# Two mixers on one core: TensorE in program order in the woven stage, the products of head pairs alternated, modulation steps two by two

## The chip, the cores and the metric

The kernel runs on one core of one Trainium2 chip. The metric is the time of one execution in microseconds (us) on the device. Names of engines: PE is TensorE, DVE is VectorE, ACT is ScalarE, POOL is GpSimd, and SP is the engine whose queue issues most of the loads.

## The reference

Two layers of a diffusion backbone run over 256 context and 256 latent tokens of width 1024. Each layer has a mixer and a mixture of experts, both behind a modulated norm. What matters here is the mixer:

```
mod = silu(c) @ w_mod[l] + b_mod[l]                  # shifts, scales, gates; the same for c_ctx
p = modnorm(x, ...) @ w_in                           # one projection for both groups
A: q, k, v of 8 heads from low-rank parts, rotary on 32 of 96 dimensions
   s = q.k ; p = softmax(s * scale) ; o_att = p @ v  # context reads context, latents read both
B: state-space mixer, two directions, chunks of 128:
   states per chunk ; y = (C B^T * decay) @ (x dt) + C exp(acs) @ h_prev + D x
   o_ssd = rmsnorm(y * silu(z))
out = concat(o_att, o_ssd) @ w_out ; x = x + gate * out
```

In layer 0 both streams leave the mixer (four tiles of 128 queries). In layer 1 only the latents do (two tiles), and their queries read all 512 keys.

## The kernel before, in words

Each mixer first projects and convolves. Then comes the stage that the change is about: three generators are woven together by `weave`. Each yields a cost after every step, and the one whose summed cost over its weight (`ATT_W`, `SSD_W`, `MOD_W`) is smallest goes next.

- **Attention, `g_att`.** A unit is a head pair's half: group `a` of two heads, query tile `t`, head `e`. `qk_proj` (L749) makes kT and qT of a pair: L753 and L760 on PE, copied out on ACT and DVE (L754, L755, L762, L763). `scores` (L766) multiplies q and k on PE (L770), then runs the softmax: maximum on DVE (L772), exponential on ACT (L774), reciprocal and scale on DVE (L775, L776). `flip` (L779) transposes the probabilities on PE (L783) and copies them to pT on ACT (L785). `attend` (L788) multiplies v by pT on PE (L792), 2 products for 256 keys (tiles 0 and 1 of layer 0), 4 for 512. Head 0 writes partitions 0 to 63 of a PSUM tile `py`, head 1 partitions 64 to 127, and one DVE copy (L821) takes the tile out. With `LOOK = 3`, step n makes the scores of unit n, flips unit n-3 and attends unit n-4.
- **State space, `g_ssd`.** Six chunk states (L891 on POOL, products L894), then for each query tile: a product (L912), masks (L917), a decay matrix per half of the heads from a broadcast load on the SP queue into `ring` (L924; L930, L934 on DVE or POOL, L936 and L943 on ACT, L938 to L944 on DVE or POOL), products with the states (L953, L955), the main product (L960), gate and norm (L961 to L967), and transposes (L972, L974).
- **Modulation, `mods`.** A chain of `mod_group` (L269) for the later parts of this layer and `mod_norm1` (L212) for the next layer's first norm. `mod_group` reads a 1 MB piece of `w_mod` per step (tile `wl`, issued at L139 on the SP queue) and multiplies it in four groups of 32 columns (L303). It ends with transposes (L316). `mod_norm1` has eight blocks; each multiplies a 1 MB piece (L221), yields, and, after a DVE copy of the result to `mr` (L223), runs a small product with a selector (L227) and three DVE instructions (L228 to L230).

The weight pieces live in a pool of `WHB = 4` buffers of 1 MB. Until the last `qk_proj`, `wkv` and `wq` hold two of them. PSUM has two buffers each for scores (`sc`), transposes (`tp`) and other products (`bk`), and one each for `py` and `md` (the modulation).

The order in which a program issues is not always the order in which an engine runs it: outside a `manual_schedule` block a scheduler sets the order on each engine. Before the change, the woven stage stands outside of such a block, so the scheduler orders PE there. The other engines and the SP queue are the scheduler's in both kernels.

## Time and profile before

| | us |
|---|---|
| median of 3 runs | 1081.5 (1081.06 to 1082.82) |
| profiled execution | 1077.21 |
| its span | 1075.4 |
| PE busy | 954.0 (89%) |
| DVE busy | 610.3 (57%) |
| POOL busy | 354.6 (33%) |
| ACT busy | 335.1 (31%) |

The profiled execution is the one that every row below is from. Its own time is 1.8 us above its span. In rows of groups, the columns are line, engine, operation, names out<-in, shapes and count, then busy time and the mean of one in ns, then the idle time in front and who ended it. In timeline rows, a start and a duration come first; the busy durations of matmuls overlap each other, so what a block of products costs PE is the step from its start to the next row's start. A product of the program is two matmuls in the trace, a transpose one.

### The profile page before, as it was taken

The page shows a single profiled execution, that of the slowest core. Times are in us where ns is not written, and L with a number is a line of the kernel's source. Part 1 is how long each engine was busy: PE and PEld are TensorE (multiplying, and loading weights), DVE is VectorE, ACT ScalarE, POOL GpSimd, SP SyncE. Part 2 cuts the span into 40 slices and gives each one's busy share as a digit, 9 for nine tenths or more (in the row PEclk, how much of TensorE's full clock was granted, in tenths as well). Part 3 has the DMA queues.
Part 4 walks back from the last instruction along what each step waited for, and adds up shares of the span by engine and source line. Part 5 has one row for each costly group of instructions (what it writes and reads, how often), then busy time and mean ns, then how long its engine had stood idle before and what let it go on. Part 6 is the DMA issues. An engine that isn't in the chain of part 4 may idle for free. (4 is left out here: it accounts for less than half of the span.)

```text
span 1075.4 us, 14508 instructions
## 1 busy us (share of the span) xinstructions
PE 954.0 (89%) x5244; PEld 556.7 (52%) x5244; DVE 610.3 (57%) x1351; ACT 335.1 (31%) x688; POOL 354.6 (33%) x366
## 2 busy tenths in 40 slices
PE   5999999999996999999969979999999678877785
PEld 3678745667775444444424327683678434433331
DVE  4587089885687355656435667857886423323232
ACT  4365344453541111111102126543455111110111
POOL 2130134430355266667645650103331001112023
PEclk9999999999996999999989989999999598899699
DMA  9512387687567989799898625646496689999995
GB/s 380 188 42 76 143 312 253 255 301 267 220 178 284 378 360 405 317 418 417 360 375 329 268 79 194 236 156 258 178 326 236 229 335 395 420 419 387 391 418 208
DMA packets 54675, 306.21 MB, mean 285 GB/s; under 512 B 6168, under 2 KB 7064, under 8 KB 22976
## 3 DMA queue, kind: packets, MB, share of 16 engines
q1 hardware_dynamic: 49120, 288.10, 68.4%
q0 software_dynamic: 4224, 15.21, 4.4%
q10 hardware_dynamic: 1248, 1.86, 0.5%
q8 instruction: 44, 0.72, 0.3%
q14 instruction: 39, 0.32, 0.1%
HBM read 300.89 MB, written 4.26 MB: 284 GB/s over the span
## 5 line engine op out<-in xcount | busy, mean ns | idle before, releaser
L1669 POOL TENSOR_TENSOR xs<-xs,tmp 128x512 f32<-128x512 f32 x144 | 180.0, 1282 | 219.6 <-DVE tmp L1668 219.5
L1604 PE MATMUL bk<-we,xgT 128*64 128x512 f32 (+1 forms) x942 | 189.6, 610 | 7.2 <-DMA we<-wgu 7.2
L1604 PEld LDWEIGHTS bk<-we,xgT 128*64 128x64 f32 (+1 forms) x942 | 51.4, 126 | 104.9 <-issue 90.2
L1653 ACT ACTIVATE yh<-sc,gs 128x512 fp32r<-128x512 f32 x46 | 31.6, 687 | 223.3 <-PE sc L1639 180.1
L1654 DVE SCALAR_TENSOR_TENSOR yl<-sc,gs,yh 128x512 fp32r<-128x512 f32 x46 | 34.4, 748 | 102.2 <-ACT yh L1653 102.2
L1639 PE MATMUL sc<-we,sa 128*64 128x512 f32 (+1 forms) x432 | 87.0, 599 | 1.1 <-DMA we<-wdn 1.1
L1578 PE MATMUL tp<-PT,h 128*128 128x128 f32 x256 | 56.4, 362 | 32.7 <-DVE xgT L1584 18.9
L1578 PEld LDWEIGHTS tp<-PT,h 128*128 128x128 f32 x256 | 43.4, 245 | 49.3 <-DVE xgT L1584 26.3
L1668 DVE TENSOR_TENSOR tmp<-md,g 128x512 f32<-128x512 f32 x60 | 41.3, 688 | 26.7 <-POOL xs L1669 22.4
L1639 PEld LDWEIGHTS sc<-we,sa 128*64 128x64 f32 (+1 forms) x432 | 26.6, 125 | 53.0 <-issue 50.4
L1668 DVE TENSOR_TENSOR tmp<-py,g 128x512 f32<-128x512 f32 x53 | 36.4, 686 | 23.9 <-PE py L1665 13.0
L770 PE MATMUL sc<-kT,qT 128*128 128x512 f32 (+1 forms) x96 | 45.7, 559 | 0.0
L792 PE MATMUL py<-pT,vt 128*64 128x128 f32 x320 | 43.6, 280 | 1.3 <-DVE oT L821 1.3
L1072 DVE TENSOR_TENSOR lo<-wo,hi 128x512 fp32r<-128x512 f32 x44 | 34.3, 784 | 16.2 <-PE sc L1255 8.6
L1584 DVE TENSOR_SCALAR xgT<-tp,a,sh 128x128 f32<-128x128 f32 x32 | 13.1, 408 | 53.0 <-PE tp L1578 53.0
L1609 ACT ACTIVATE sa<-bk 128x256 f32<-128x256 f32 x24 | 9.2, 383 | 106.0 <-PE bk L1604 106.0
L792 PEld LDWEIGHTS py<-pT,vt 128*64 128x64 f32 x320 | 32.6, 136 | 15.5 <-issue 8.2
L401 PE MATMUL bk<-wh,hH 128*128 128x256 f32 (+1 forms) x128 | 39.8, 311 | 0.2
L774 ACT ACTIVATE p<-sc,mx 128x512 f32<-128x512 f32 (+1 forms) x48 | 29.4, 612 | 33.7 <-DVE mx L772 26.8
L403 PE MATMUL bk<-wh,hL 128*128 128x256 f32 (+1 forms) x128 | 38.1, 298 | 1.8 <-DVE hL L382 1.7
L1582 ACT ACTIVATE xgT<-tp,sh,a 128x128 f32<-128x128 f32 x32 | 14.6, 457 | 80.2 <-PE tp L1578 80.2
L402 PE MATMUL bk<-wl,hH 128*128 128x256 f32 (+1 forms) x128 | 37.8, 295 | 0.0
(417 smaller groups left out, 2169.3 us busy)
## 6 DMA issues: line engine op xcount, KB each, us to landing
we<-wgu SPq DMA_DIRECT2D x111, 1024.0 KB, 13.9
we<-wdn SPq DMA_DIRECT2D x53, 1024.0 KB, 12.2
wl<-wmod SPq DMA_DIRECT2D x22, 1024.0 KB, 5.0
wl<-wm SPq DMA_DIRECT2D x10, 1024.0 KB, 8.2
wo<-wout SPq DMA_DIRECT2D x8, 1024.0 KB, 5.7
ring<-wgu SPq DMA_DIRECT2D x7, 1024.0 KB, 20.0
we<-wgu SPq DMA_DIRECT2D x27, 256.0 KB, 5.4
wm<-wm SPq DMA_DIRECT2D x6, 1024.0 KB, 12.2
```

The lines of the kernel that those rows point to most:

```text
L401: T.matmul(o, a[0], b[0], start=start, stop=False)
L402: T.matmul(o, a[0], b[1], start=False, stop=False)
L403: T.matmul(o, a[1], b[0], start=False, stop=stop)
L770: T.matmul(pm[:, 0:nk], qT[:, e, t * 128:(t + 1) * 128], kT[:, e, 0:nk], start=True, stop=True)
L792: T.matmul(py[e * 64:(e + 1) * 64, 0:128], vts[0][:, k, h * 64:(h + 1) * 64], pT[:, k * 128:(k + 1) * 128], start=(k == 0), stop=(k == nk ...
L1072: eng.tensor_tensor(lo, src, hi.bitcast(F32), op=ALU.subtract)
L1578: T.matmul(p_, R["hres"][t][:, c], xg[j], start=(j == 0), stop=(j == nT - 1))
L1604: T.matmul(pg[c], xgT[b][part][:, k, c], w[i][k], start=(part == 0 and k == 0), stop=(part == 1 and k == 3))
L1639: T.matmul(pd[h][c], aT[:, k, c], w[i][2 * k + h], start=(k == 0), stop=(k == 1))
L1654: V.scalar_tensor_tensor(yl, pd[h], gs[:, b:b + 1], yh.bitcast(F32), op0=ALU.mult, op1=ALU.subtract)
L1668: V.tensor_tensor(tmp, pc, g2[1 if t < 2 else 0][h], op=ALU.mult)
L1669: (eng or (V if EADD[l][n] == "V" or alt and n % 2 else G)).tensor_tensor(xs[:, t, hs_], xs[:, t, hs_], tmp, op=ALU.add)
```

## The change

1. `attend` takes both heads of a pair and alternates between them at each block of 128 keys. The copy L821 moves into it.
2. `g_att` goes by pairs. Per pair n: `qk_proj` of pair n+2 where it is new, attend of pair n-1, then for each head the scores of pair n+1 and the flip of pair n. `LOOK` is gone.
3. `double` joins two yields of the modulation chain into one step.
4. The costs that `g_ssd` yields become 1.0, 0.4 and 1.4.
5. The weave stands inside `tc.manual_schedule(engines=ME)`, with `ME` holding PE alone: PE runs this stage in program order.

The number of instructions and the bytes moved are the same.

```diff
-LOOK = 3
...
+
+    def double(g):
+        for c in g:
+            yield c + next(g, 0.0)
 
     def drain(g):
         for _ in g:
@@ -785,42 +788,47 @@
             S.activation(pT[:, 0:nk], pt[:, 0:nk], AF.Copy)
             return pT
 
-        def attend(a, t, e, pT, py):
-            h = 2 * a + e
+        def attend(a, t, pT):
+            py = py_()
             nk = 256 if t < 2 else 512
             for k in range(nk // 128):
-                T.matmul(py[e * 64:(e + 1) * 64, 0:128], vts[0][:, k, h * 64:(h + 1) * 64], pT[:, k * 128:(k + 1) * 128],
-                         start=(k == 0), stop=(k == nk // 128 - 1))
+                for e in range(2):
+                    h = 2 * a + e
+                    T.matmul(py[e * 64:(e + 1) * 64, 0:128], vts[0][:, k, h * 64:(h + 1) * 64], pT[e][:, k * 128:(k + 1) * 128],
+                             start=(k == 0), stop=(k == nk // 128 - 1))
+            V.tensor_copy(otile(0, t)[:, a], py[:, 0:128])
 
         def g_att():
-            units = [(a, t, e) for a in range(4) for t in qtiles for e in range(2)]
+            units = [(a, t) for a in range(4) for t in qtiles]
             kq = {0: qk_proj(0)}
             yield 4.3
             ps_, pTs = {}, {}
-            py = None
-            for n in range(len(units) + LOOK + 1):
-                c = 0.0
-                if n < len(units):
-                    a, t, e = units[n]
-                    if a not in kq:
-                        kq[a] = qk_proj(a)
-                        yield 4.3
-                    ps_[n] = scores(kq[a], t, e)
-                    c += 0.86 if t >= 2 else 0.43
-                m = n - LOOK
-                if 0 <= m < len(units):
-                    pTs[m] = flip(units[m][1], ps_.pop(m))
-                    c += 0.43 if units[m][1] >= 2 else 0.22
-                m -= 1
-                if m >= 0:
-                    a, t, e = units[m]
-                    if e == 0:
-                        py = py_()
-                    attend(a, t, e, pTs.pop(m), py)
-                    if e == 1:
-                        V.tensor_copy(otile(0, t)[:, a], py[:, 0:128])
-                    c += 0.5 if t >= 2 else 0.25
-                yield c
+
+            def score(n, e):
+                a, t = units[n]
+                ps_[n, e] = scores(kq[a], t, e)
+                return 0.86 if t >= 2 else 0.43
+
+            yield score(0, 0)
+            yield score(0, 1)
+            for n in range(len(units) + 1):
+                nxt = n + 1 < len(units)
+                if n + 2 < len(units) and units[n + 2][0] not in kq:
+                    a = units[n + 2][0]
+                    kq[a] = qk_proj(a)
+                    yield 4.3
+                if n:
+                    a, t = units[n - 1]
+                    attend(a, t, [pTs.pop((n - 1, e)) for e in range(2)])
+                    yield 0.5 if t >= 2 else 0.25
+                for e in range(2):
+                    c = 0.0
+                    if nxt:
+                        c += score(n + 1, e)
+                    if n < len(units):
+                        pTs[n, e] = flip(units[n][1], ps_.pop((n, e)))
+                        c += 0.43 if units[n][1] >= 2 else 0.22
+                    yield c
 
         dts = cut(spt, 256, 64, "p (t h) -> p t h", t=4)
         wdt = cut(spt, 320, 64, "p (t h) -> p t h", t=4)
@@ -943,7 +951,7 @@
                     S.activation(Lt, Lt, AF.Exp)
                     (G if MG[l][g] == "G" else V).tensor_tensor(w_, w_, Lt, op=ALU.mult)
                     Ms[g] = w_
-                    yield 0.1
+                    yield 1.0
                 for d in range(2):
                     if (d, t) not in hprev:
                         continue
@@ -954,7 +962,7 @@
                     yi = P.tile([128, 520], F32, tag="xp", name="yi", bufs=2)[:, 0:512]
                     V.tensor_tensor(heads(yi), heads(pi), hb(eac[:, 0, t, 8 * d:8 * d + 8]), op=ALU.mult)
                     G.tensor_tensor(yt, yt, yi, op=ALU.add)
-                    yield 0.86
+                    yield 0.4
                 py = bk()
                 for h in range(8):
                     T.matmul(py[:, h * 64:(h + 1) * 64], Ms[h // 4][:, h % 4], xt[:, t, h * 64:(h + 1) * 64], start=True, stop=True)
@@ -965,8 +973,7 @@
                 S.activation(junk, yt, AF.Square, accum_out=sy)
                 ry = rstd_of(sy, 1, 512)
                 S.activation(yt, yt, AF.Copy, scale=ry)
-                yield 1.75
-                yield 0.01
+                yield 1.4
                 pt = tp()
                 for b in range(4):
                     T.transpose(pt[:, b * 128:(b + 1) * 128], yt[:, b * 128:(b + 1) * 128], ident)
@@ -988,7 +995,8 @@
         drain(g_k())
         drain(g_v())
         load_ahead(l, 3)
-        weave((g_att(), ATT_W[l]), (g_ssd(), SSD_W[l]), (mods, MOD_W[l]))
+        with tc.manual_schedule(engines=ME):
+            weave((g_att(), ATT_W[l]), (g_ssd(), SSD_W[l]), (double(mods), MOD_W[l]))
 
         return [o.rearrange("p (k t) -> p k t", k=8) for o in oTs]
 
```

Where the order moves. The rows are PE's, in the order in which PE runs them; a row names the line, the names out<-in, the shape of one product and how many follow each other. Lines after the change are shifted: L302, L220 and L226 are the modulation products (before: L303, L221, L227), L773 the scores (L770), L786 the flip (L783), L797 the attend (L792), L902 the states (L894), L920 and L961 the state-space products (L912, L953). An `x8` of L302 is a double step, an `x4` of L303 a single one.

Layer 0, PE, the modulation steps early in the stage. Before, with the scores of the first units and the states:

```order
L303 MATMUL md<-wl,kc 32x512 x7
L770 MATMUL sc<-kT,qT 128x256 x2
L894 MATMUL bk<-xw,bcb 64x256 x4
L770 MATMUL sc<-kT,qT 128x256
L894 MATMUL bk<-xw,bcb 64x256 x2
L770 MATMUL sc<-kT,qT 128x256
L783 MATMUL tp<-kc,p 128x128 x4
L770 MATMUL sc<-kT,qT 128x512
L303 MATMUL md<-wl,kc 32x512 x4
L792 MATMUL py<-pT,vt 64x128 x2
L770 MATMUL sc<-kT,qT 128x512
```

After, the first two steps:

```order
L302 MATMUL md<-wl,kc 32x512 x8
L902 MATMUL bk<-xw,bcb 64x256 x4
L773 MATMUL sc<-kT,qT 128x256
L302 MATMUL md<-wl,kc 32x512 x8
L773 MATMUL sc<-kT,qT 128x256 x2
```

After, the third and fourth step:

```order
L302 MATMUL md<-wl,kc 32x512 x8
L902 MATMUL bk<-xw,bcb 64x256 x4
L797 MATMUL py<-pT,vt 64x128 x4
L773 MATMUL sc<-kT,qT 128x512
L786 MATMUL tp<-kc,p 128x128 x4
L302 MATMUL md<-wl,kc 32x512 x8
```

Before, single steps stand a dozen rows apart; after, steps one and two have only states and one score between them, and steps three and four have states, an attend, a score and a flip.

Layer 0, PE, the attends of the third and fourth pair of the first group (512 keys). Before, one row or half of one per head:

```order
L316 MATMUL tp<-kc,bm 128x128 x4
L303 MATMUL md<-wl,kc 32x512 x4
L783 MATMUL tp<-kc,p 128x128 x4
L912 MATMUL bk<-bcb 128x256
L953 MATMUL bk<-hs,bcb 128x256
L770 MATMUL sc<-kT,qT 128x512
L792 MATMUL py<-pT,vt 64x128 x2
L303 MATMUL md<-wl,kc 32x512 x4
L972 MATMUL tp<-kc,yt 128x128 x4
L783 MATMUL tp<-kc,p 128x128 x2
L792 MATMUL py<-pT,vt 64x128 x2
L770 MATMUL sc<-kT,qT 128x512
```

After:

```order
L773 MATMUL sc<-kT,qT 128x512
L786 MATMUL tp<-kc,p 128x128 x4
L302 MATMUL md<-wl,kc 32x512 x8
L920 MATMUL bk<-bcb 128x256
L773 MATMUL sc<-kT,qT 128x512
L786 MATMUL tp<-kc,p 128x128 x4
L797 MATMUL py<-pT,vt 64x128 x8
L773 MATMUL sc<-kT,qT 128x256
L786 MATMUL tp<-kc,p 128x128 x4
L773 MATMUL sc<-kT,qT 128x256
L786 MATMUL tp<-kc,p 128x128 x4
L797 MATMUL py<-pT,vt 64x128 x8
```

Before, an attend stands behind its own flip by two rows or more, or mixed with other products; after, each `L797 x8` holds both heads and stands directly behind the flip of the second.

Layer 0, PE, blocks of `mod_norm1` near the stage's end. Before:

```order
L227 MATMUL tp<-kc,mr 128x2 x2
L221 MATMUL md<-wl,kc 32x256 x8
L770 MATMUL sc<-kT,qT 128x256
L783 MATMUL tp<-kc,p 128x128 x2
L792 MATMUL py<-pT,vt 64x128 x4
L960 MATMUL bk<-xt,W 128x64 x2
L960 MATMUL bk<-xt,U 128x64 x4
L770 MATMUL sc<-kT,qT 128x512
L783 MATMUL tp<-kc,p 128x128 x2
L792 MATMUL py<-pT,vt 64x128 x2
L227 MATMUL tp<-kc,mr 128x2 x2
L221 MATMUL md<-wl,kc 32x256 x8
```

After:

```order
L220 MATMUL md<-wl,kc 32x256 x8
L226 MATMUL tp<-kc,mr 128x2 x2
L920 MATMUL bk<-bcb 128x256
L773 MATMUL sc<-kT,qT 128x512
L786 MATMUL tp<-kc,p 128x128 x4
L797 MATMUL py<-pT,vt 64x128 x8
L220 MATMUL md<-wl,kc 32x256 x8
L226 MATMUL tp<-kc,mr 128x2 x2
L786 MATMUL tp<-kc,p 128x128 x8
L797 MATMUL py<-pT,vt 64x128 x8
```

Before, other work stands between L221 and its L227; after, L226 follows L220 at once, and the attend follows the flip at once.

## Rows read from the trace of the kernel before

**Rows 1.** Page, part 1: busy time of each engine over the span.
```profile
span 1075.4 us, 14508 instructions
PE 954.0 (89%) x5244; PEld 556.7 (52%) x5244; DVE 610.3 (57%) x1351; ACT 335.1 (31%) x688; POOL 354.6 (33%) x366
```

**Rows 2.** Windows: length, busy PE, PEld, DVE, ACT, POOL, granted clock, DMA share, GB/s.
```profile
123.00:262.00 139.00, 136.34 (x833) 76.88 (x832) 106.02 (x278) 66.89 (x173) 43.55 (x46) 1.00 0.72 264
727.00:805.30 78.30, 74.81 (x438) 45.92 (x438) 62.91 (x142) 36.21 (x88) 27.09 (x28) 1.00 0.68 249
...
360.00:540.00 180.00, 175.73 (x804) 75.07 (x802) 98.59 (x171) 25.92 (x44) 112.90 (x93) 1.00 0.94 378
880.00:1020.00 140.00, 111.57 (x688) 55.14 (x680) 43.28 (x87) 17.93 (x35) 25.48 (x21) 0.85 0.98 403
```

**Rows 3.** Groups of PE in 123:262 (layer 0): busy, mean ns, idle before and releaser.
```profile
L792 PE MATMUL py<-pT,vt 128*64 128x128 f32 x180 | 26.5, 282 | 1.3 <-DVE oT L821 1.3
L303 PE MATMUL md<-wl,kc 128*32 128x512 f32 x128 | 18.9, 604 | 0.0
```

**Rows 4.** Groups of PE in 727:805.3 (layer 1), same columns.
```profile
L760 PE MATMUL bk<-kvqa,wl 128*128 128x256 f32 x28 | 7.4, 394 | 1.3 <-DVE yi L955 0.7 <-DVE kT L755 0.5
L953 PE MATMUL bk<-hs,bcb 128*128 128x256 f32 x16 | 4.3, 392 | 1.1 <-DVE qT L763 1.1
```

**Rows 5.** Timeline of PE: start, duration, line, shapes, count; attends of one head.
```profile
140.14 0.65 PE L792 MATMUL py<-pT,vt 128*64 128x128 f32 x4
140.72 1.12 PE L770 MATMUL sc<-kT,qT 128*128 128x512 f32 x2
...
159.56 1.09 PE L792 MATMUL py<-pT,vt 128*64 128x128 f32 x8
160.58 0.70 PE L770 MATMUL sc<-kT,qT 128*128 128x256 f32 x2
```

**Rows 6.** Timeline of PE at the end of layer 0's stage.
```profile
261.59 1.58 PE L792 MATMUL py<-pT,vt 128*64 128x128 f32 x16
263.10 1.08 PE L1038 MATMUL md<-ke,sh 128*128 128x36 f32 x8
```

**Rows 7.** Timeline of PE at the start of layer 0's stage.
```profile
131.80 1.92 PE L303 MATMUL md<-wl,kc 128*32 128x512 f32 x14
133.65 1.13 PE L770 MATMUL sc<-kT,qT 128*128 128x256 f32 x4
134.71 1.08 PE L894 MATMUL bk<-xw,bcb 128*64 128x256 f32 x8
135.72 0.70 PE L770 MATMUL sc<-kT,qT 128*128 128x256 f32 x2
```

**Rows 8.** Timeline, all engines, near the stage's end: a flip, its copy, the modulation copy.
```profile
258.35 0.66 PE L783 MATMUL tp<-kc,p 128*128 128x128 f32 x4
258.48 0.42 DVE L223 COPY mr<-md 128x256 f32<-128x256 f32 x1 [0.30 <-PE md L221]
259.96 0.66 PE L783 MATMUL tp<-kc,p 128*128 128x128 f32 x4
260.37 0.48 PE L1255 MATMUL bk<-hi 128*128 128x512 f32 x1
260.71 0.60 ACT L785 ACTIVATE pT<-tp 128x512 f32<-128x512 f32 x1 [0.49 <-PE tp L783]
```

**Rows 9.** Groups of ACT in 123:262: the copy of 256 keys.
```profile
L785 ACT ACTIVATE pT<-tp 128x256 f32<-128x256 f32 x16 | 6.0, 380 | 12.1 <-PE tp L783 11.9
```

**Rows 10.** Timeline of the SP queue, and the loads of tile wl from issue to landing.
```profile
132.91 1.19 SPq L139 DMA_DIRECT2D wl<-wmod  x2
...
DMA to landing us min/median/max: 5.0/6.3/7.7
```

**Rows 11.** Timeline of DVE: the two batches of the state-space part.
```profile
190.51 1.14 DVE L934 SCALAR_TENSOR_TENSOR Lt<-ring,sact,Lt 128x128 f32<-128x128 f32 x4 [0.48 <-POOL Lt L930]
...
231.70 3.53 DVE L938 SCALAR_TENSOR_TENSOR U<-sml,sact,U 128x128 f32<-128x128 f32 x4
```

## The prediction

> **What bounds the kernel now.** I read the page's busy times first, then windows around the two stages that the change touches, then the groups of those windows, then single timeline rows. TensorE (PE) is busy 89% of the span [rows 1], so what counts is where PE could finish sooner. The woven stages, where attention, the state-space part and the modulation share the engines, are 123 to 262 us (layer 0) and 727 to 805.3 us (layer 1). In the first PE is busy 136.34 of 139.00 us, in the second 74.81 of 78.30 [rows 2]: PE is the bound, at a granted clock of 1.00, with 2.7 and 3.5 us idle. VectorE (DVE) is second, at 106.02 and 62.91 us. Of PE's groups, the attends (L792) waited 1.3 us in all in layer 0 and the modulation products (L303) 0.0 [rows 3]: the scheduler's order leaves nothing between a product and its data. Layer 1's small waits are for DVE [rows 4]. So PE's time there can fall only through less PE work, and an order that no longer fits the data shows as idle PE at once. What follows each stage depends on its result; in layer 0 the experts fill PE again (175.73 of 180 us), in layer 1 the loads fill the DMA (0.98) [rows 2], and I let every microsecond of a stage pass to the end one to one.
>
> **Part 1: the products of a head pair together.** A head's attend costs 0.58 us of PE for 256 keys (140.14 to 140.72) and 1.02 for 512 (159.56 to 160.58) [rows 5]. Now two heads alternate, each writing its 64 partitions. For what alternation gives there are two kinds of row. Of the same line, one group of 16 matmuls in which the two heads happened to follow each other took 1.51 us (261.59 to 263.10) instead of 2.04 [rows 6]: a gain of 0.53 per pair. Of another line that alternates strictly between two groups of 64 columns, eight state products (L894) took 1.01 us, where four full-width scores of the same 256 elements took 1.06 [rows 7]: 0.126 against 0.265 us each, so half. I take the half, because strict alternation is what the change writes; the bound below is 0.53 for 512 keys and half of it for 256. Layer 0 has 8 pairs of each kind: 8 x 1.02 + 8 x 0.58 = 12.8, less the 0.5 that the row of 16 has already, is **-12.3** (bound -5.9). Layer 1 has 8 pairs of 512 and two such rows of 16: 8.2 - 1.0 = **-7.2**. [...]
>
> One copy of the output per pair stays as it was, and so do bytes and instruction count. The modulation steps two by two give PE nothing: fourteen products in a row took 1.85 us (0.132 each) [rows 7].
>
> **Part 2: attends directly behind their flips.** In program order PE cannot take other work while an attend waits. The order of the changed kernel puts 9 of layer 0's 16 attends directly behind the second head's transposes, 5 of them with 512 keys. The price: transposes at 259.96, PE free for its next work at 260.37, the copy of pT on ScalarE from 260.71 to 261.31 [rows 8]: 0.94 us of wait. For 256 keys the copy is 0.38 instead of 0.60 [rows 9]: 0.72. So 5 x 0.94 + 4 x 0.72 = **+7.6**. In layer 1 three attends stand so (+2.8) and one has only a state product of 0.58 between (+0.4).
>
> **Part 3: the small modulation product behind its own copy.** Two by two, the product with `sel` (L227) comes behind the big one in the same step, 7 times of 8 with nothing between. It needs the copy on DVE: PE took its next work at 258.35, the copy ended at 258.90 [rows 8]: 0.55 us. 7 x 0.55 = **+3.9**, in layer 0 alone.
>
> **Part 4: the modulation weights.** While `wkv` and `wq` are held, two of the four 1 MB buffers remain. A double step reads both, and the load for the next step starts when the first half is through: step at 131.80, load issued at 132.91 [rows 7, 10]; loads land after 5.0, 6.3 or 7.7 us (minimum, median, maximum) [rows 10]. Before, single steps stood wherever their load had landed. Now between steps one and two stand only state products (1.01) and one score (0.53): PE is there at 133.65 + 1.01 + 0.53 = 135.2 and the data at 139.2, a wait of 4.0 (2.7 to 5.4). Between steps three and four stand 1.01 + 0.58 + 0.96 + 0.53 = 3.1 us of work; counted from the step's start, PE is there at 2.0 + 3.1 = 5.1, the data at 1.1 + 6.3 = 7.4: 2.3 (1.0 to 3.7). Other steps are far enough apart. **+6.3** (3.7 to 9.1). On the SP queue six weight loads now stand ahead of the first `ring<-ad` load; its use lies some 30 us later, so I cost this at nothing.
>
> **Part 5: softmax late behind the state-space part.** The look-ahead falls from three heads to one pair, and DVE now holds batches of the state-space part between the reduce and the scale of a softmax that PE waits for. Such a batch takes 1.14 us (four L934) or 3.53 us (four L938) [rows 11]. DVE's 106.02 us over 16 pairs are 6.6 us per pair, so it has little room. I take one short batch per 128-row tile: 4 x 1.14 = **+4.6** in layer 0 (0 to 4 x 3.53 = 14.1), 2 x 1.14 = +2.3 in layer 1 (0 to 7.1). `qk_proj` moving two pairs ahead I cost at nothing: both kT buffers are free by then and PE does the same work.
>
> **The sum.** Of today's idle time I let half vanish into these waits: -1.4 and -1.7. Layer 0: -12.3 + 7.6 + 3.9 + 6.3 + 4.6 - 1.4 = +8.7. Layer 1: -7.2 + 2.8 + 0.4 + 2.3 - 1.7 = -3.4. Together +5.3 on the profiled execution, whose 1077.21 us lie 4.3 under the median of the runs; I add the difference to the median: 1081.5 + 5.3 = 1086.8, rounded to **1087**. About 0.2% (2.2 us) is what a measurement of this kernel can tell from no change.
>
> **Rivals.**
> - **Only the forced waits remain; faster.** The credit is whole, softmax is never late (Part 5 is zero), the loads land at their fastest (3.7), and today's idle goes. Layer 0: -12.3 + 7.6 + 3.9 + 3.7 - 2.7 = +0.2; layer 1: -7.2 + 2.8 - 3.5 = -7.9. That is 1081.5 - 7.7 = **1074**. For it: each forced wait gives DVE and ScalarE time to catch up, and ScalarE is busy only 66.89 us of 139 [rows 2]. It decides once late softmax costs under about 3 us in both layers together. Against it: the DVE room above.
> - **DVE sets the pace; much slower.** Each tile holds a softmax back by the long batch: Part 5 becomes 14.1 + 7.1 instead of 6.9, so 1087 + 14.3 = **1101**. For it: DVE's 106 us would have to fit about 125 us of PE work. [...]
> - **Balance.** Credits and waits cancel within 2.2 us: 1081.5.
> - **The products do not overlap.** If each weight load held up the other head's products, the 19.5 us of credit vanish: 1087 + 19.5 = **1106**. Rows 6 and 7 speak against it.
>
> **Chances and range.** Forecast case (slower by 2.2 to about 11 us) 0.41; only forced waits 0.35; balance 0.12; DVE's pace 0.08; no overlap 0.04. So faster 0.35, same 0.12, slower 0.53. The range takes in the faster rival with about 3 us beyond it, and upward the loads at their slowest (+2.8) and half of what Part 5 could add: 1071 to 1097. The likeliest case alone spans 1084 to 1093.
>
> **What would show each step.** Part 1: the group of attends at half its spacing, pairs of 512 keys in about 1.0 us; at 1.5 us or more the credit was too large. Parts 2 and 3: idle before the attends with the copy of pT as releaser, about 8 us in layer 0, and about 4 before the small product with the mr copy as releaser. Part 4: idle before the modulation products with a DMA as releaser, two waits of 2 to 4 us. Part 5: idle before the transposes with the scale on DVE as releaser. PE's busy time in the two stages should fall by about 19 us together; the first stage should last about 148 us, the second about 75. The prediction is wrong if these waits are under half as long, or fall on the same microseconds, so that the first stage ends before 139 us.

## The result, and the profile after

The changed kernel takes 1110.3 us (median of 4 runs, 1105.6 to 1116.9), the kernel before, measured beside it, 1081.3. The ratio is 1.029 [1.026, 1.033]: slower by some 29 us of measured time, where 5.5 were forecast and the range ended at 1097. The profiled execution has a span of 1108.6 us, 33.2 more than the one of before, which was itself 4 us faster than its median.

```profile
span 1108.6 us, 14504 instructions
PE 947.7 (85%) x5244; PEld 549.5 (50%) x5244; DVE 608.2 (55%) x1351; ACT 334.6 (30%) x688; POOL 354.0 (32%) x366
```

PE's busy time fell by 6.3 us in all against [rows 1], where 19 were forecast for the two stages alone, and the program is longer. Where the 33.2 us lie, from the first and last products of each stage in the two traces (us):

| stretch | before | after | difference |
|---|---|---|---|
| up to the first `qk_proj` of layer 0 | 125.2 | 122.4 | -2.8 |
| from there to the last attend | 138.0 | 155.4 | +17.4 |
| from there to the end of the output products | 61.7 | 70.5 | +8.8 |
| router, experts, layer 1 up to its first `qk_proj` | 399.1 | 402.3 | +3.2 |
| from there to the last attend of layer 1 | 81.4 | 84.8 | +3.4 |
| from there to the end of the output products | 21.5 | 24.8 | +3.3 |
| the rest | 248.5 | 248.4 | -0.1 |

The first row lies ahead of all that was changed; over all the profiled executions of this document it ranges from 120.7 to 125.6. The stage of layer 0 and its tail hold 26 us, layer 1's 7.

These windows of the changed kernel, with the columns of [rows 2], are the stage of layer 0 and four stretches in it:

```profile
122.40:277.80 155.40, 124.62 (x771) 70.02 (x774) 97.66 (x260) 62.79 (x166) 38.61 (x41) 0.92 0.62 229
178.00:186.00 8.00, 5.77 (x17) 2.74 (x16) 5.89 (x12) 4.61 (x11) 2.03 (x3) 0.79 0.77 325
222.00:230.00 8.00, 7.45 (x42) 4.12 (x41) 3.63 (x13) 2.40 (x8) 3.93 (x5) 0.70 0.51 187
238.00:245.00 7.00, 7.00 (x35) 5.72 (x32) 4.10 (x12) 1.92 (x5) 0.85 (x1) 0.58 0.27 114
252.00:260.00 8.00, 8.00 (x46) 5.57 (x45) 3.42 (x9) 3.05 (x10) 0.75 (x2) 0.65 0.13 55
```

PE is busy 124.6 of 155.4 us. It stands 30.8 us, where the kernel before stood 2.7 in 139 [rows 2]. And its granted clock is no longer 1.00: in the four stretches it is 0.58 to 0.79, and in three of them PE is at work nearly all the time. I estimate the loss as (1 - clock) x busy, from the products behind the longest wait below: four matmuls took 3.78 us at a granted clock of 0.50 and 1.88 at 1.00. That gives 0.21 x 5.8 + 0.30 x 7.5 + 0.42 x 7.0 + 0.35 x 8.0 = 9.2 us. VectorE is busy 97.7 us of the longer stage, a smaller share than before; over the whole stage it does not set the pace by its amount of work.

What PE waited for most in layer 0's stage and tail (us in total, times, longest):

```profile
PE md L302 <- DMA wl<-wmod: 8.3, 6, 1.9
PE bk L763 <- DVE kT L758: 5.8, 2, 5.2
PE tp L226 <- DVE mr L222: 5.1, 6, 2.4
PE py L797 <- ACT pT L788: 3.8, 8, 1.2
PE tp L226 <- ACT p L777: 2.9, 1, 2.9
```

The kernel before had 1.3 us in front of its attends and 0.0 in front of its modulation products [rows 3]. Two of them by groups (columns as in [rows 3]):

```profile
L797 PE MATMUL py<-pT,vt 128*64 128x128 f32 x192 | 19.2, 301 | 4.1 <-ACT pT L788 3.8
L763 PE MATMUL bk<-kvqa,wl 128*128 128x512 f32 x32 | 18.5, 720 | 7.4 <-DVE kT L758 5.8 <-DVE yt L969 1.7
```

The attends' busy time is 19.2 us, where the kernel before spent 26.5 [rows 3, which hold 180 of the 192]. The q products' mean is 720 ns, where the same line has 602 at a granted clock of 1.00 (`e1_sched`); here the clock is 0.53 from 182.38 to 186.00 and 0.50 from 221.58 to 225.36, two stretches of such products behind a wait. Two rows of the timeline show the pair at a granted clock of 1.00 (249.27 to 250.30):

```profile
249.27 1.09 PE L797 MATMUL py<-pT,vt 128*64 128x128 f32 x16
250.30 0.84 PE L773 MATMUL sc<-kT,qT 128*128 128x256 f32 x2
```

Sixteen matmuls of a pair take 1.03 us. One head alone took 1.02 [rows 5]. This is a pair whose probabilities had arrived. Nine of layer 0's 16 pairs wait, as this one does:

```profile
162.55 0.43 PE L797 MATMUL py<-pT,vt 128*64 128x128 f32 x2
163.37 1.09 PE L797 MATMUL py<-pT,vt 128*64 128x128 f32 x14 [0.38 <-ACT pT L788]
164.38 0.70 PE L773 MATMUL sc<-kT,qT 128*128 128x256 f32 x2
```

From its first product to the next work it holds PE for 1.83 us, because the second head's probabilities come late. Of these 0.80 us of wait the list of waits counts 0.38: the first two matmuls count as busy for 0.43.

The longest wait, in the timeline of all engines:

```profile
213.24 1.07 ACTq L293 DMA_DIRECT2D bm<-bmod  x2
214.55 1.88 PE L763 MATMUL bk<-kvqa,wl 128*128 128x512 f32 x4
219.52 0.69 DVE L306 TENSOR_TENSOR bm<-md,bm 128x512 f32<-128x512 f32 x1 [4.97 <-DMA bm<-bmod]
220.83 0.69 DVE L758 COPY kT<-bk 64x512 f32<-64x512 f32 x1
221.58 3.78 PE L763 MATMUL bk<-kvqa,wl 128*128 128x512 f32 x4 [5.15 <-DVE kT L758]
```

PE finished the first head's q products and stood 5.15 us for the copy of kT, which frees the PSUM buffer of the second. That copy (L758) was ready to run early, but on VectorE it is queued behind L306, the sum of the modulation and its bias rows, and L306 waited 4.97 us for the load of these rows (L293), issued at 213.24. After the wait the same four matmuls take 3.78 us instead of 1.88: the granted clock is 0.50 from 221.58 to 225.36, where it was 1.00 from 214.55 to 216.43.

### The profile page after: what moved, and what is told of

It reads as the page before. It is cut to its first block, busy times and chain, and to the rows that moved or that the text cites. A ratio compares the mean times of both kernels' runs of the same rounds, so it can differ in the third digit from the quotient of the medians.

```text
span 1108.6 us, 14504 instructions
## 1 busy us (share of the span) xinstructions
PE 947.7 (85%) x5244; PEld 549.5 (50%) x5244; DVE 608.2 (55%) x1351; ACT 334.6 (30%) x688; POOL 354.0 (32%) x366
## 5 line engine op out<-in xcount | busy, mean ns | idle before, releaser
L1612 PE MATMUL bk<-we,xgT 128*64 128x512 f32 (+1 forms) x942 | 193.4, 627 | 5.7 <-DMA we<-wgu 5.7
L773 PE MATMUL sc<-kT,qT 128*128 128x512 f32 (+1 forms) x96 | 47.4, 579 | 0.0
L1080 DVE TENSOR_TENSOR lo<-wo,hi 128x512 fp32r<-128x512 f32 x44 | 34.2, 783 | 13.7 <-PE sc L1263 6.0
L404 PE MATMUL bk<-hH,wh 128*128 128x512 f32 (+1 forms) x96 | 37.8, 394 | 0.0
L406 PE MATMUL bk<-hH,wl 128*128 128x512 f32 (+1 forms) x96 | 37.1, 386 | 0.3 <-POOL wl L385 0.3
```

The source lines that it names most:

```text
L404: T.matmul(o, a[0], b[0], start=start, stop=False)
L406: T.matmul(o, a[1], b[0], start=False, stop=stop)
L773: T.matmul(pm[:, 0:nk], qT[:, e, t * 128:(t + 1) * 128], kT[:, e, 0:nk], start=True, stop=True)
L1080: eng.tensor_tensor(lo, src, hi.bitcast(F32), op=ALU.subtract)
L1612: T.matmul(pg[c], xgT[b][part][:, k, c], w[i][k], start=(part == 0 and k == 0), stop=(part == 1 and k == 3))
```

## The experiments

Theory A, formed on this trace: the program order on PE costs, because PE now stands wherever one input is late, and its clock falls behind these waits. Rivals: B, the double modulation steps; C, the new costs of the state-space part; and that the alternated products cost or save more than thought. Ratios are to the kernel before, measured on the same chip at the same time, with 95% intervals.

| PE's order in the weave | products | modulation | attention, costs | ratio |
|---|---|---|---|---|
| program (the change) | pairs | double | by pairs, new | 1.029 [1.026, 1.033] |
| scheduler (`e1_sched`) | pairs | double | by pairs, new | 1.002 [1.000, 1.005] |
| program (`e2_single`) | pairs | single | by pairs, new | 1.018 [1.014, 1.021] |
| program (`e3_heads`) | heads | double | by pairs, new | 1.038 [1.035, 1.041] |
| program (`e4_oldcost`) | pairs | double | by pairs, old | 1.030 [1.028, 1.033] |
| scheduler (`e5_sched_oldcost`) | pairs | double | by pairs, old | 0.998 [0.995, 1.001] |
| scheduler (`e6_before_pair`) | pairs | single | before, old | **0.988** [0.985, 0.992] |
| program (`e9_before_order`) | heads | single | before, old | 1.032 [1.029, 1.035] |
| scheduler (`e10_pair_double`) | pairs | double | before, old | 0.999 [0.997, 1.001] |
| program (`e12_pair_order`) | pairs | single | before, old | 1.013 [1.010, 1.015] |

**The scheduler's order back (`e1_sched`).**

```diff
-        with tc.manual_schedule(engines=ME):
-            weave((g_att(), ATT_W[l]), (g_ssd(), SSD_W[l]), (double(mods), MOD_W[l]))
+        weave((g_att(), ATT_W[l]), (g_ssd(), SSD_W[l]), (double(mods), MOD_W[l]))
```

> The changed kernel with one thing undone: the weave stands outside the manual_schedule block, so the scheduler orders PE again; pairs, double steps and the new costs stay. Theory A (the program order on PE is what costs: PE stands before data that are late, and its clock falls behind these waits): the 31 us of idle PE in layer 0's stage fall to under 8, the granted clock there is 1.00 again, the attends keep their halved cost, and the time is 1062 to 1078 us, below the kernel before. Rival B (the double modulation steps cost, whoever orders PE): DMA waits in front of the modulation products stay above 5 us and the time stays above 1095 us. Rival C (the new costs of the state-space part put it at the end): the stage's tail stays late and the time stays above 1090 us.

Measured: 1.002. Nearly all of the loss goes with one line, but no gain is left. Windows of this run, the stage up to its last attend and from there to the end of the output products:

```profile
122.20:250.00 127.80, 123.89 (x792) 65.71 (x791) 93.82 (x258) 62.01 (x164) 39.76 (x42) 1.00 0.70 263
250.00:322.30 72.30, 67.20 (x331) 54.20 (x331) 51.04 (x106) 31.76 (x65) 29.84 (x31) 0.91 0.65 235
```

The stage lasts 127.8 us instead of 138.0, at a clock of 1.00 and with 3.9 us idle, as theory A has it. Then 72.3 us pass instead of 61.7: the state-space part ends at 263.7, 13.7 us after the last attend, and the output products end behind it, at a clock of 0.91. The 10 us that the stage gained are given back there, by work that moved behind the last attend and by the lower clock (by the same estimate 0.09 x 67.2 = 6.0 us). A is right on the waits and the clock, C on the late tail, and neither on the time: 1.002 is 1084 us on the scale of 1081.3, above A's window and below B's and C's. The order costs 2.7% (29 us). Whether the late tail is why no gain is left is asked in `e5_sched_oldcost`.

**Single modulation steps (`e2_single`).** `double(mods)` becomes `mods`.

> The changed kernel with single modulation steps, PE still in program order. Theory A (program order, whatever stands in it): waits move, but the kT and softmax waits stay; 1090 to 1105 us. Rival B (the double steps): the DMA waits (8.3 us), the waits of the small modulation product (8.0) and the wait behind the bias load (5.2) go, and with them most of the time at a lower clock (about 10): 1075 to 1087 us.

Measured: 1.018, some 1100 us on the scale of 1081.3: inside A's window, outside B's. The waits of this run:

```profile
PE bk L763 <- DVE kT L758: 4.4, 3, 2.3
PE py L797 <- ACT pT L788: 4.1, 8, 1.5
...
PE md L302 <- DMA wl<-wmod: 1.1, 2, 0.6
```

The waits for the weights fall from 8.3 to 1.1 us and those of the small product vanish from the list; the waits for kT and for pT stay. The double steps hold about 12 of the 29 us (1.029 against 1.018).

**Heads one after the other (`e3_heads`).**

```diff
-            for k in range(nk // 128):
-                for e in range(2):
-                    h = 2 * a + e
+            for e in range(2):
+                h = 2 * a + e
+                for k in range(nk // 128):
```

> The changed kernel with one head after the other inside each attend; the order of everything else stays. If alternating the heads is worth the halved products (12 us in layer 0, 7 in layer 1) also here, where PE waits often: 1122 to 1132 us. If the waits behind it take the gain up (what PE saves, it waits): 1108 to 1118 us. If alternating costs (the products hold each other up): under 1105 us.

Measured: 1.038, some 1122 us on that scale, at the edge of the first window. But this run undoes less than its expectation takes it to: the two heads still stand directly behind each other. From its trace, a pair of 512 keys that does not wait; the score behind it takes 0.70 us, as in [rows 5]:

```profile
198.70 1.58 PE L797 MATMUL py<-pT,vt 128*64 128x128 f32 x16
200.21 0.70 PE L773 MATMUL sc<-kT,qT 128*128 128x256 f32 x2
```

It takes 1.51 us, where the alternated one takes 1.03 and two heads apart take 2.04; with 256 keys both orders take 0.6. So the alternation itself is worth at most 16 x 0.48 = 7.7 of the 19.5 us here, and standing together gives the rest. By the ratios alternating saves 9 us, give or take some 5. The two traces show nothing of it in layer 0 (225.8 us from the first `qk_proj` to the end of the output products, against 225.9) and 3.2 us in layer 1 (112.8 against 109.6).

**The old costs (`e4_oldcost`).** The three new yields of `g_ssd` go back.

> The changed kernel with the state-space part's old costs (0.1, 0.86, 1.75 and 0.01), so that its steps come at other places. Rival C (the new costs push the state-space part behind the attention, so that the output products wait some 9 us in layer 0 and some 3 in layer 1): 1093 to 1101 us. Theory A: the waits move, the sum stays: 1104 to 1118 us, or more, as the new costs may have been the better fit.

Measured: 1.030, no difference to the changed kernel, and inside A's window. In layer 0 the last attend comes later (280.5 instead of 277.8), the state-space part sooner, and from the first `qk_proj` to the end of the output products it is 226.4 us instead of 225.9. So the new costs are not what makes the changed kernel slow.

**The scheduler's order and the old costs (`e5_sched_oldcost`).**

> Pairs and double steps, but the scheduler orders PE and the state-space part has its old costs. In the run without the manual_schedule block the last attend of layer 0 came 10 us sooner after the stage's start than in the kernel before, and the output products ended no sooner, because the state-space part ended late. Theory A1 (the gain of the pairs is there and was given back at the state-space tail): the state-space transposes of layer 0 end within 132 us of the stage's start (before: 126, without the block: 141), the output products end 4 to 9 us sooner than before, and the ratio to the kernel before is 0.990 to 0.996. Rival A2 (VectorE, at 106 of 139 us before, sets the pace once PE needs less): the tail stays late and the ratio is 0.998 to 1.005.

Measured: 0.998 [0.995, 1.001], between the two windows. The tail part of A1 holds: the state-space transposes end 131.8 us after the stage's start. But the output products end only 0.8 us sooner than before (198.9 after the start against 199.7). What takes the rest is the question of the two runs with the order of before.

**The pairs alone (`e6_before_pair`).** The kernel before, with `attend` of the change, called when the second head's turn comes:

```diff
-                if m >= 0:
+                if m >= 0 and units[m][2] == 1:
                     a, t, e = units[m]
-                    if e == 0:
-                        py = py_()
-                    attend(a, t, e, pTs.pop(m), py)
-                    if e == 1:
-                        V.tensor_copy(otile(0, t)[:, a], py[:, 0:128])
-                    c += 0.5 if t >= 2 else 0.25
+                    attend(a, t, [pTs.pop(m - 1), pTs.pop(m)])
+                    c += 1.0 if t >= 2 else 0.5
```

> The kernel before with one thing changed: the attends of a pair are issued together with alternating heads, when the second head's turn comes; look-ahead of three heads, single modulation steps, old costs and the scheduler's order stay. If the halved products pay where nothing else moves: layer 0's stage 6 to 12 us shorter, ratio 0.988 to 0.995. If layer 1's gain is lost in the experts that wait for their loads, and layer 0's behind VectorE: 0.997 to 1.003. If the pair's second attend now holds PSUM and probabilities longer and that costs: over 1.003.

Measured: 0.988 [0.985, 0.992], 1067.8 us: faster than both kernels. Its two stages, to their last attends:

```profile
122.10:252.30 130.20, 127.24 (x850) 69.92 (x849) 100.69 (x279) 64.88 (x170) 43.56 (x46) 1.00 0.76 278
713.00:790.80 77.80, 74.25 (x448) 42.94 (x447) 60.83 (x144) 39.07 (x90) 27.23 (x28) 0.98 0.74 272
```

Layer 0's stage is 130.2 us instead of 138.0, at a clock of 1.00; its output products end 7.8 us sooner. In layer 1 they end 3.6 us sooner, and the rest of the program takes 3.9 us more than before. That is no sign that the experts of layer 1 take the gain back: in the profiled executions of this document the stretch from there to the end takes 248.1 to 255.5 us, whatever the stage did (255.5 in `e9_before_order`, whose layer 1 is longer). The medians differ by 11.4 us, as much as the two gains together (7.8 + 3.6).

**The bias rows loaded early (`e7_bias_early`).** `BMK = 6` becomes 2: the load L293 is issued at the chain's third piece.

> The changed kernel with the bias rows of the modulation loaded at the chain's piece 2 instead of piece 6; nothing else. Theory A (one late 8 KB load holds VectorE for 5 us, the kT copy behind it, and so PE): PE's longest wait in layer 0 (5.15 us in front of the second q products) falls under 1.5 us, the granted clock behind it is higher, and the ratio to the kernel before is 1.018 to 1.025. Rival (VectorE is late there anyway; the wait only changes its name): the idle time of the stage stays at 30 us and the ratio at 1.027 to 1.031.

Measured: 1.024 [1.020, 1.029], inside A's window, though the interval reaches the rival's. The waits of this run:

```profile
PE tp L226 <- DVE mr L222: 5.8, 6, 2.7
...
PE tp L226 <- ACT p L777: 5.3, 1, 5.3
...
PE bk L763 <- DVE kT L758: 0.8, 2, 0.6
```

The wait for kT is gone (0.8 us in all), and a part of it stands elsewhere: in front of the small modulation product, the wait that was 2.9 us is 5.3. The clock behind the place is higher, as A has it: 1.00, where the changed kernel had 0.70.

```profile
222.00:230.00 8.00, 6.35 (x60) 3.46 (x58) 7.26 (x16) 3.04 (x9) 4.72 (x5) 1.00 1.00 421
```

**The wait filled with work (`e8_fill`).** Five products are added where PE stood.

```diff
+                if ctx_out and a == 3 and e == 0:
+                    fill = tp()
+                    for _ in range(5):
+                        T.matmul(fill, wkv[:, a * 128:(a + 1) * 128], kvaT, start=True, stop=True)
```

> The changed kernel with five products of 128x512 more (4.8 us of PE, into a spare PSUM tile that nobody reads) in the place where PE stood 5.15 us in layer 0, between the two heads' q products of the last pair group. If the granted clock fell there because PE stood: it stays at 1.00 through the products that follow, for some 15 us, and the time falls by 2 to 5 us although PE does more (ratio to the kernel before 1.024 to 1.028). If the clock falls for another reason: it falls all the same, and the time stays or rises by up to 4 us (1.029 to 1.033).

Measured: 1.033 [1.028, 1.037]. The clock answers as the first of the two says, the time as the second. Windows of this run:

```profile
216.00:222.00 6.00, 6.00 (x16) 2.76 (x17) 1.84 (x2) 2.61 (x6) 0.99 (x3) 1.00 0.90 354
222.00:230.00 8.00, 6.49 (x37) 3.10 (x35) 5.55 (x16) 1.13 (x4) 0.62 (x1) 1.00 0.61 225
```

The granted clock is 1.00 and 1.00; in the changed kernel the second of these stretches had 0.70, and PE's four products after the wait took 3.78 us, where they take 1.98 here. So at this place the clock fell where PE stood and stayed at 1.00 where PE had work, and the time was not saved all the same. The clock of 1.00 lasted 8 of the 15 us that were expected: it was 0.93 from 230 to 238 and, behind the next wait, 0.59 from 238 to 245. From the timeline of this run:

```profile
219.58 4.46 PE L767 MATMUL tp<-kvqa,wl 128*128 128x512 f32 x10
224.66 1.98 PE L763 MATMUL bk<-kvqa,wl 128*128 128x512 f32 x4 [0.63 <-DVE kT L758]
...
239.56 0.99 PE L226 MATMUL tp<-kc,mr 128*128 128x2 f32 x4 [4.74 <-ACT p L781]
```

The next wait, in front of the small product (L226), is 4.74 us where it was 2.91. The row names ScalarE, whose exponential ended at the same moment; what L226 reads is the copy `mr` on VectorE, which ended just before (239.42). Counted from the first `qk_proj`, PE came 0.6 us sooner and that copy 1.3 us later. What no row bears out is that the price of the lower clock can be had back: here the following wait took it.

**Program order alone (`e9_before_order`).** The kernel before, its weave inside `tc.manual_schedule(engines=ME)`.

> The kernel before with the manual_schedule block around its weave and nothing else: heads one by one, look-ahead of three heads, single modulation steps, old costs, but PE in program order. Theory A (program order on PE is what costs, whatever the order written is): idle PE of 20 to 40 us in layer 0's stage, a granted clock under 0.97, ratio 1.020 to 1.040. Rival (the order of the changed kernel costs: pairs with a short look-ahead, double steps; a look-ahead of three heads would bear program order): ratio 0.998 to 1.010.

Measured: 1.032 [1.029, 1.035]. The windows of its two stages:

```profile
122.20:272.80 150.60, 138.58 (x840) 81.19 (x839) 104.56 (x276) 65.83 (x170) 42.98 (x46) 0.95 0.69 250
734.10:830.30 96.20, 81.68 (x448) 49.71 (x447) 63.13 (x144) 39.14 (x90) 27.33 (x28) 0.95 0.59 220
```

PE stands 12.0 and 14.5 us, at a clock of 0.95, with the long look-ahead and with nothing else changed. The idle time is less than I gave to theory A (20 to 40), the ratio is in its window. The waits are others than in the changed kernel: the longest in layer 0 are 4.3 us in front of the transposes of the modulation and 2.9 for a state-space step on VectorE.

**Pairs and double steps under the scheduler (`e10_pair_double`).**

> The faster kernel of the round before (the kernel before with the pairs' attends alternated, ratio 0.988) with the modulation steps two by two. The scheduler orders PE. If the double steps cost only where PE keeps program order: ratio 0.985 to 0.991, no change. If two 1 MB pieces per step cost under the scheduler too (the DMA waits): 0.993 to 1.000, which would explain the 0.998 of the run with pairs, double steps and old costs; if not, that run's loss lies in the order by pairs and its short look-ahead.

Measured: 0.999 against 0.988 without the double steps: they cost 1.1% under the scheduler too. One place shows how:

```profile
178.26 1.06 PE L303 MATMUL md<-wl,kc 128*32 128x512 f32 x8 [0.41 <-DMA wl<-wmod]
184.61 1.93 PE L303 MATMUL md<-wl,kc 128*32 128x512 f32 x8 [3.04 <-DMA wl<-wmod]
```

PE waits 0.4 and 3.0 us for pieces of the weights, where the kernel before waited 0.0 [rows 3] and the pairs alone 0.5. The run with pairs by pairs, the scheduler and the old costs has one such wait of 1.8 us. So double steps are enough to take the pairs' gain away; how the rest of the 1.1% comes about is not taken apart here.

**The attends behind the next score (`e11_attend_late`).** In the changed kernel, the attend of pair n-1 moves behind the first score of pair n+1.

> The changed kernel with each attend issued behind the first score of the next pair, instead of in front of it, so that 0.5 to 1.0 us of PE work stands between a flip and its attend. If the attends' waits for pT are time lost (3.8 us in layer 0, 2.2 in layer 1 in the changed kernel): they fall under 1.5 us together and the ratio to the kernel before is 1.022 to 1.027. If VectorE and ScalarE set the pace, so that PE waits elsewhere instead: the waits for pT fall and others grow, ratio 1.027 to 1.034.

Measured: 1.022 [1.019, 1.025], at the lower edge of the first window. The waits of this run:

```profile
PE tp L226 <- DVE mr L222: 9.0, 7, 2.4
PE md L302 <- DMA wl<-wmod: 6.1, 5, 1.4
...
PE py L797 <- ACT pT L788: 1.2, 3, 0.5
```

The waits for pT fall from 3.8 to 1.2 us in layer 0 and from 2.2 to 0.5 in layer 1 (1.7 together, not quite under 1.5), and others grow little. Some 8 us of the 29 are gone. That is more than the list of waits had, which shows only about half of a pair's wait.

**Pairs and program order (`e12_pair_order`).**

> The kernel before with the pairs' attends alternated (ratio 0.988) and PE in program order in the weave; old look-ahead, single steps, old costs. Theory A: program order costs 15 us or more here too, ratio 1.005 to 1.030. Rival: the order written by heads with a look-ahead of three bears program order, ratio 0.986 to 1.000. The difference to the changed kernel (1.029) is what double steps, the order by pairs and the new costs add under program order.

Measured: 1.013. Its two stages:

```profile
124.00:264.20 140.20, 126.22 (x846) 72.69 (x845) 102.94 (x276) 64.61 (x170) 42.97 (x46) 0.95 0.70 256
724.50:815.50 91.00, 74.00 (x448) 43.86 (x447) 63.41 (x144) 38.93 (x90) 28.06 (x28) 0.94 0.62 233
```

Theory A's window holds. Against 0.988 with the scheduler, program order costs 2.4% (26 us) here. PE stands 14.0 us in layer 0's stage and 17.0 in layer 1's. Against `e9_before_order` the pairs save 2.0% (19.2 us between the medians): under program order with the long look-ahead their whole credit arrives. From here to the changed kernel, the order by pairs with the new costs adds 0.5% (`e2_single`, 1.018) and the double steps 1.2%. The shorter look-ahead was not changed alone.

## Why the prediction was wrong, step by step

The direction was right, the size was not: 5.5 us were forecast, 29 measured. Two terms that the sum put at nothing failed it: the granted clock, which by my estimate cost PE 9.2 us of busy time in layer 0 and 3.9 in layer 1, and the waits of `qk_proj` for VectorE, 8.0 us. Beside them Part 3 was short by 4.1 us, and layer 1 was taken for a gain.

- **Part 1 was right in its price.** A pair of 512 keys takes 1.03 us instead of 2.04 where it does not wait. What gives it is not alternation alone: one head behind the other takes 1.51 in `e3_heads`, as in [rows 6], and two heads of 256 keys take 0.6 in either order. Worth on the clock: 11.4 us where the scheduler keeps PE's order (`e6_before_pair`), 19.2 under program order with the old look-ahead (`e12_pair_order` against `e9_before_order`).
- **Part 2 was right too, though the list of waits shows half of it.** 7.6 us were taken for layer 0, and the list has 3.8, because a pair's first two matmuls count as busy. I add up every attend of layer 0 from its first product to the next work, with the waits in front: 22.2 us. Without a wait they would take 8 x 1.03 + 8 x 0.59 = 13.0, and the lower clock makes some 1.6 of it, an estimate. That leaves 7.6 us of wait, at nine attends, five of them with 512 keys, as forecast. In the kernel before the same sum is 25.9, so Parts 1 and 2 together saved 3.7 us where 4.7 were forecast.
- **Part 3 was half of what came.** 3.9 us against 8.0 (5.1 and 2.9 in the waits). I priced the copy to `mr` from [rows 8], where VectorE was free. The five plain cases cost 0.55 as priced; two cost 2.4 and 2.9, because the copy stood in VectorE's queue behind steps of the state-space part and of softmax. Before the longer of the two waits VectorE was at work without a gap, 7.29 us of the 8 from 230 to 238. L946 is a state-space step:

```profile
230.90 2.47 DVE L946 SCALAR_TENSOR_TENSOR U<-sml,sact,U 128x128 f32<-128x128 f32 x2
233.90 0.60 DVE L946 SCALAR_TENSOR_TENSOR U<-sml,sact,U 128x128 f32<-128x128 f32 x2
236.90 0.83 PE L226 MATMUL tp<-kc,mr 128*128 128x2 f32 x4 [2.91 <-ACT p L777]
```

  The same two steps took 2.47 us while GpSimd was at work (its steps run from 230.84 to 233.23) and 0.60 just after it. That GpSimd slows them was not tested.
- **Part 4 was right.** 6.3 us against 8.3. The two places named cost 2.5 and 2.6 (4.0 and 2.3 forecast); a third, which I held for far enough apart, 3.3. These are the second and the third, each step's two pieces apart:

```profile
157.07 1.07 PE L302 MATMUL md<-wl,kc 128*32 128x512 f32 x8 [1.07 <-DMA wl<-wmod]
159.63 1.06 PE L302 MATMUL md<-wl,kc 128*32 128x512 f32 x8 [1.49 <-DMA wl<-wmod]
...
195.89 1.06 PE L302 MATMUL md<-wl,kc 128*32 128x512 f32 x8 [1.86 <-DMA wl<-wmod]
198.35 1.06 PE L302 MATMUL md<-wl,kc 128*32 128x512 f32 x8 [1.40 <-DMA wl<-wmod]
```

- **Part 5 named the mechanism at the wrong place.** Waits in front of flips are 1.5 us in layer 0. The waits for VectorE came at `qk_proj` instead, which I costed at nothing because its buffers of kT are free: 5.8 + 1.7 + 0.5 = 8.0 us. The buffer that was not free was PSUM's, freed by a copy at the end of VectorE's queue. The bias load behind the longest one was in no part of the sum, although the diff joins the chain's last two pieces in one step, and the load is issued at the first of them.
- **The largest term that was missing is the granted clock.** I read 1.00 in [rows 2], and gave the waits their own length as their price. Products behind the two longest waits of layer 0 ran at a lower clock (0.50 behind 5.15 us, and 0.50 from 237.66 to 239.56 behind 2.91); over the four stretches above I estimate 9.2 us more of PE's time in layer 0; in layer 1 it fell to 0.85 and 0.63 in the two stretches of 10 us from 800 to 820, another 1.1 + 2.8 = 3.9 us by the same working. What this is worth in time is not shown: where the wait was filled and the clock so kept for that stretch (`e8_fill`), the kernel was no faster.
- **Layer 1 was forecast as a gain.** -3.4 was the sum, +6.7 was measured. Its stage has 13.8 us of idle PE (70.98 busy of 84.80) against 3.5, in many waits of 2.2 us at most, where Parts 2 and 5 had 5.5 for it.
- **The end of a stage is its latest part, not its last attend.** The new costs were taken as a rearrangement only. The state-space part of layer 0 ends 41 us later than before (transposes until 292.9 instead of 251.5), 15 us after the last attend, and the stretch up to the end of the output products grew by 8.8. With the old costs (`e4_oldcost`) the tail is shorter and the stage longer by as much.
- **One to one was not refuted for layer 1.** The time behind it varies by 7 us between executions, more than its gain in any run.

In layer 0's stage the parts added 7.6 + 3.9 + 6.3 + 4.6 - 1.4 = 21.0 us of waits. The measured stage, beside this row of the kernel before:

```profile
125.20:263.20 138.00, 135.34 (x841) 77.29 (x840) 106.19 (x278) 65.37 (x170) 43.55 (x46) 1.00 0.72 264
```

PE stands 28.1 us more (30.8 against 2.7) and is busy 10.7 us less (124.6 against 135.3): together the 17.4 measured. What makes up the 10.7 can be estimated only: the pairs save 12.3, less some 4 of their waits that count as busy; the clock adds 9.2; the rest, some 12, is work that lies behind the last attend now (771 matmuls in the stage against 841).

Of the rivals, that of products which do not overlap came nearest in time (1106), and its mechanism did not happen: a pair takes 1.03 us. The one with VectorE's pace (1101) has a part of the mechanism. Over the stage VectorE worked 97.7 of 155.4 us, so its order made PE wait, not its whole load; in places, as in front of the late copy to `mr`, it was full (7.29 of 8 us). The longest wait, 5.15 us, was one for a copy out of PSUM (kT, L758), but for its place in VectorE's queue, and no run here shows the amount of such copies as the bound: where the scheduler kept PE's order, the stage shrank by 8 to 10 us with VectorE at 73 to 77% of it.

## What to carry to other kernels

On an engine that is busy 98% of a stage [rows 2], a program order must keep work between every product and its slowest input, or leave the order to what knows the waits; here that alone was worth 2.4 to 3.2%, whichever order was written. Look at the clock behind a wait on TensorE (here 0.50 behind one of 5.15 us), and follow the queue of the engine that ends it: an 8 KB load held VectorE for 4.97 us, a copy behind it, and so PE. Hold a list of waits against the starts in the timeline. Take a change apart before it is dropped: its one good part was worth 1.2%.

## What the runs showed of the hardware that I had not expected

- A wait of 5.15 us was followed by products at a granted clock of 0.50 (3.78 us for four matmuls instead of 1.88 at 1.00); with the wait filled with products (`e8_fill`) the clock was 1.00 from 222 to 230, instead of 0.70.
- Two heads of 64 columns each took, with 512 keys and their products alternating, 1.03 us for sixteen matmuls, against 1.51 for one head behind the other and 1.02 for the eight of one head.
- In program order the profile's waits of PE (31 us in layer 0's stage) do not show all of the loss: the 9.2 us that I estimate for the lower clock stand in no list of waits, and of the 7.6 us that attends waited the list has 3.8.
